# Five K pairs with seven products in nine gate/up chunks, with two weight rests per chunk on GpSimd

## The chip, the cores and the metric

The kernel runs on one core of one Trainium2 chip. The metric is the device time of one execution in microseconds, taken as the median of several runs. Before the change it is 2190.61 us (three runs, 2189.62 to 2191.96).

The engines are named as the profile names them: PE is TensorE (matrix products) and PEld its weight load, DVE the vector engine, ACT ScalarE, POOL GpSimd, SP the engine whose queue issues most transfers.

## The reference

A trunk of two layers over 256 tokens of width 2048, in float32. Each layer has a mixer (one input projection, eight heads of stick-breaking attention, eight of differential attention, one output projection) and a SwiGLU feed-forward of width 5632:

```python
for l in range(DEPTH):
    h = rms_norm(x, pre_mix_norm[l])
    m = hybrid_mixer(h, l, w_in[l], w_o[l], ...)
    x = x + rms_norm(m, post_mix_norm[l])
    h = rms_norm(x, pre_ffn_norm[l])
    f = swiglu(h, w_gate[l], w_up[l], w_down[l])
    x = x + rms_norm(f, post_ffn_norm[l])

def swiglu(h, w_gate, w_up, w_down):
    return (jax.nn.silu(h @ w_gate) * (h @ w_up)) @ w_down
```

The change concerns `h @ w_gate` and `h @ w_up`, matrices of 2048 x 5632 each.

## The kernel before

**Precision.** A float32 operand is split into a rounded part `hi` and a rest `lo` = operand - `hi`, and a product is three matmuls: hi x hi, hi x lo and lo x hi (function `product`, lines 1116 to 1118). For each weight tile of 128 x 1024, ScalarE writes `hi` (line 351) and the vector engine the rest `lo` (line 354). The rest reads two tiles in SBUF, `raw` and `hi`.

**Tiling.** The 5632 columns of gate and up are walked in eleven chunks of 512 (loop variable `c`, 0 to 10; the text calls them first to eleventh). In a chunk, K = 2048 is walked in eight pairs `kp` of two 128-row tiles. Tokens are two tiles of 128. So a pair of one chunk is a 2 x 2 block product for gate and up at once: eight products (function `eight`) or, with sums of blocks, seven (function `seven`, which calls `seven_products`). Which pairs take the second form says `gate_sevens(c)`: pairs 2, 4, 5, 6 (`SEVEN`) as a rule, 2 to 6 (`MORE_SEVEN`) in the chunks of `MORE_AT`, fewer in the first two.

**What a pair in seven products needs.** In place of two raw tiles it has `G` (gate) and `T` (up). SP's queue loads both. GpSimd issues a further transfer that adds the first half of the gate tile to the first half of `T` on the way (line 298). `feed` then takes the gate tile through lines 351 and 354 as any weight, and `mixed_weights` does the rest for the up tile: hi and lo of `T` (lines 319, 320); T's second half minus its first, in place (334); that difference added to both halves of `G`, in place (335); hi and lo of the difference (`Th`, `Tl`, 128 x 512) and of the new `G` (128 x 1024). On the token side it needs sums of token blocks, made once per layer and pair by `pair_sums` and placed by `FORM_AT`: a pair (chunk, position) gives the K pair whose sums are made there. Pairs 4, 6, 5, 2 get theirs in the first two chunks, pair 3 in the fifth.

For two pairs (3 and 5) in each of the eighth and tenth chunk the weight sums were made ahead, during the mixer's end (`foresee`, `FORESEEN`), and come back from DRAM.

**Chunk end.** After the last pair in seven products the shared sums leave PSUM (`shared_part`: line 1157 on ScalarE, 1158 to 1161 on the vector engine), after the last pair come lines 1308 to 1311 (sum, SiLU, product), and some ticks later transposes into `act` (1317, 1318).

**Order.** The program is recorded in the order of the Python code; a scheduler then orders each engine's instructions by priority and sets the semaphores. Each engine runs its queue in that order. Weights are fed four ahead of their use (`LOOKAHEAD`), the accumulating transfer of a `T` is recorded up to four weights before that (`EARLY`). There are four `raw` tiles, six `hi` and six `lo`, three `G`, four `T`, two each of `Th` and `Tl`. GpSimd's queue in the gate/up stage holds the accumulating starts and nothing else.

**x.** The residual x lies in four quarters in `rooms` (tag `late`, four places). They are written to DRAM one by one by `put_away`, in the second position of the chunks in `AWAY_AT`, which frees the places for later tiles, among them the token sums of pair 3 (`ss`).

Of the kernel before, what the change touches and what calls it, by code (L numbers as in the profile page):

```python
# [9 lines left out]
F32 = mybir.dt.float32  # L10
# [3 lines left out]
ALU = mybir.AluOpType  # L14
# [10 lines left out]
FF = 5632  # L25
CW = 512
# [18 lines left out]
FIRST_ORDER = (0, 1, 3, 2, 7, 4, 6, 5)  # L45
NEXT_SEVEN = (4, 5, 6)
MORE_SEVEN = (2, 3, 4, 5, 6)
MORE_AT = (7, 9)
FORESEEN = {7: (3, 5), 9: (3, 5)}
AHEAD_AT = 8  # L50
AHEAD_PACE = 2
FORM_AT = {(0, 1): 4, (0, 2): 6, (0, 5): 5, (1, 3): 2, (4, 3): 3}
DOWN_SEVEN = ((4, 7, 10, 12, 15, 17, 20), (3, 5, 8, 10, 13, 15, 18))

WARM = 10
LEVEL = 232
EARLY = 4
LEAD = 6
AWAY_AT = (3, 4, 5, 6)
X_BACK = 12  # L60


# [7 lines left out]
def gate_sevens(c):  # L70

    if c in MORE_AT:
        return MORE_SEVEN
# [3 lines left out]
def weight_order():  # L77

    order = []

    def queue_pair(name, l, kp, c):
        order.append((name, l, kp, c))
        return len(order) - 1

    plan = []
    sevens, plain, own = set(), set(), set()
    for l in range(L):
        lay = {"in": {}, "o": {}, "gate": {}, "up": {}, "down": {}}
        for n, (ca, cb) in enumerate(PAIRS):
            for kp in IN_ORDER if n else range(KT // 2):  # L90
                lay["in"][ca, kp] = queue_pair("w_in", l, kp, ca)
                lay["in"][cb, kp] = queue_pair("w_in", l, kp, cb)
                if kp in IN_NOW[n]:
                    plain.add(lay["in"][cb, kp])
        order_o = [(c, kp) for kp in KP_O for c in (0, 1)]
        order_o += [(c, kp) for kp in LATE_O for c in (2, 3)] + [(c, kp) for c in (2, 3) for kp in LAST_O]
        lay["order_o"] = order_o
        for c, kp in order_o:
            lay["o"][c, kp] = queue_pair("w_o", l, kp, c)
            if c == 3 and kp in O_SEVEN:  # L100
                own.add(lay["o"][c, kp])
        for c in range(FF // CW):
            for kp in FIRST_ORDER if c == 0 else range(KT // 2):
                lay["gate"][c, kp] = queue_pair("w_gate", l, kp, c)
                lay["up"][c, kp] = queue_pair("w_up", l, kp, c)
                if kp in gate_sevens(c):
                    sevens.add(lay["up"][c, kp])
        for half in range(2):
            for kp in range(FF // P // 2):
                for c in (2 * half, 2 * half + 1):  # L110
                    lay["down"][c, kp] = queue_pair("w_down", l, kp, c)
                if kp in DOWN_SEVEN[half]:
                    sevens.add(lay["down"][2 * half + 1, kp])
        plan.append(lay)
    return order, plan, sevens, plain, own
# [48 lines left out]
def kernel(  # L164
# [15 lines left out]
    nc = tc.nc  # L180
# [18 lines left out]

    order, plan, sevens, plain, own = weight_order()  # L200
    stream = [weights_in_turn[i].rearrange("p (k n) -> p k n", k=2) for i in range(len(order))]

    ready = {}
    raws, loads = [], []
    fed = [0]

    def fetch(upto):
        while len(raws) < min(upto, len(stream)):
            i = len(raws)
            for j in range(i, min(i + EARLY + 1, mix_raw[3])):  # L210
                if j in sevens and j not in sums and not (j in foreseen and j > i + 1):
                    summed(j)
            if i in sevens:
                raws.append(sums[i])
                continue
            if i + 1 in sevens:
                g = mix_raw[0].tile([P, 2, CW], F32, tag="G", bufs=mix_raw[1], name=f"G{i}")
                with not_ahead(i):
                    loads.append(nc.sync.dma_start(g, stream[i]))
                raws.append(g)  # L220
                continue
            if i in own or i + 1 in own:
                raw = mix_pool[0].tile([P, 2, CW], F32, tag="v", bufs=2, name=f"V{i}")
            elif i in plain or i + 1 in plain:
                raw = late_room([P, 2, CW], f"GU{i}")
            else:
                raw = wpool.tile([P, 2, CW], F32, tag="raw", bufs=4, name=f"raw{i}")
            mixing = bool({i, i + 1} & (own | plain))
            with not_ahead(i) if mixing else nullcontext():
                loads.append(nc.sync.dma_start(raw, stream[i]))  # L230
            raws.append(raw)
            if not mixing:
                usual.append((i, loads[-1]))
# [107 lines left out]
    def feed(upto):  # L341
        fetch(upto)
        while fed[0] < min(upto, len(stream)):
            i = fed[0]
            raw = raws[i]
            if i in sevens or i in plain or i in own:
                ready[i] = mixed_weights(i)
                fed[0] += 1
                continue
            hi = wpool.tile([P, 2, CW], F32R, tag="hi", bufs=6, name=f"hi{i}")  # L350
            nc.scalar.activation(hi, raw, AF.Copy)  # L351
            lo = wpool.tile([P, 2, CW], F32R, tag="lo", bufs=6, name=f"lo{i}")
            with behind():
                rest = nc.vector.tensor_tensor(out=lo, in0=raw, in1=hi.bitcast(F32), op=ALU.subtract)  # L354
            ready[i] = (hi, lo)
            fed[0] += 1
            rests.append(rest)
# [4 lines left out]
    def behind():  # L362

        if held[1] == 0:
            return nullcontext()
        held[1] -= 1
        return tc.issue_after(held[0].ins)

    def after_rests():

        return tc.issue_after(rests[-1].ins)
# [5 lines left out]
    def weights(i, ahead):  # L377
        feed(i + 1 + ahead)
        return ready[i]
# [20 lines left out]
    def put_away(nm, n):  # L400

        if n == 0:
            away.append(kept.tile([P, NT, D], F32, name=f"away_{nm}"))
        t, h = divmod(n, 2)
        with in_turn():
            nc.sync.dma_start(away[-1][:, t, h * D // 2 : (h + 1) * D // 2], xs[t][h])
# [760 lines left out]
    for l in range(L):  # L1167
# [17 lines left out]
        for n, (c, kp) in enumerate(plan[l]["order_o"][:16]):  # L1185
# [5 lines left out]
            if n in (9, 11):  # L1191
                kp = O_SEVEN[(n - 9) // 2]
# [4 lines left out]
        for kp in LATE_O:  # L1197
            i, j = (plan[l]["o"][c, kp] for c in (2, 3))
# [6 lines left out]
            hi, lo = weights(i, LOOKAHEAD)  # L1205
# [13 lines left out]
        with tc.manual_schedule(engines={mybir.EngineType.Activation, mybir.EngineType.DVE}):  # L1219
            feed(idx + 6)  # L1220
            for n, (c, kp) in enumerate(last_o):
                unit({0: accs[c, 0]}, mix, idx + n, kp, (0,), False, kp == LAST_O[-1], 0)
                if kp == LAST_O[-1]:
                    evac_sum(pool, accs[c, 0], mg, ssm, gpost, c, 0, f"o{l}")
            rescale(mg, ssm, 0, f"o{l}")
            for n, (c, kp) in enumerate(last_o):
                feed(idx + 7 + n)
                fetch(min(idx + 12 + n, idx + 12))
                unit({1: accs[c, 1]}, mix, idx + n, kp, (1,), False, kp == LAST_O[-1], 0)
                transposed(0, 32 + l * KT, xT, cols=(n,))  # L1230
                if (c, kp) == (2, LAST_O[-1]):
                    evac_sum(pool, accs[2, 1], mg, ssm, gpost, 2, 1, f"o{l}", True)
# [17 lines left out]
        def pair_sums(kp):  # L1250
            f = pool.tile([P, 2, S], F32, tag="t2", name=f"f{l}_{kp}")
            for kk in range(2):
                st = xT[2 * kp + kk]
                nc.vector.tensor_tensor(out=f[:, kk, :], in0=st[:, 0, :].bitcast(F32), in1=st[:, 1, :].bitcast(F32), op=ALU.add)
            forms[kp] = token_sums(pool, gu if kp in SEVEN else None, len(SEVEN), f[:, 0, 0:P], f[:, 1, 0:P], f[:, 0, P:S], f[:, 1, P:S], f"{l}_{kp}")
# [18 lines left out]
        for c in range(FF // CW):  # L1274
# [9 lines left out]
            for n, kp in enumerate(order):  # L1284
                if n == 1 and c in AWAY_AT:
                    put_away(f"ffn{l}", AWAY_AT.index(c))
                if (c, n) in FORM_AT:
                    with after_rests():
                        pair_sums(FORM_AT[c, n])
                if kp not in mine:  # L1290
# [41 lines left out]
        for half in range(2):  # L1332
# [74 lines left out]
            for t in range(NT):  # L1407
# [4 lines left out]
                for c in cc:  # L1412
                    for kp in range(nkp - tail, nkp):
# [3 lines left out]
                        hi, lo = weights(plan[l]["down"][c, kp], LOOKAHEAD)  # L1417
# [66 lines left out]
```

## Time and profile before

| | us |
|---|---|
| median of three runs | 2190.61 (2189.62 to 2191.96) |
| span of the profiled execution | 2189.2 |
| TensorE busy | 2174.7 (99%) |
| vector engine busy | 1921.7 (88%) |
| ScalarE busy | 1378.0 (63%) |
| GpSimd busy | 144.2 (7%) |
| ten gate/up chunks (second to eleventh), first layer | 418.3 |
| ten gate/up chunks, second layer | 419.0 |

How to read the profile. A group of instructions is a line of the kernel, an engine, an operation and its tiles (`lo<-raw,hi`: the output, then the inputs), their shape, a count, the busy time in us and the mean of one in ns, and behind the bar the idle time of that engine just before them with what ended it. A row of the order of time has the start in us, the duration in us, engine, line, operation; in brackets the idle time before it. A row of a table of stretches has the stretch, its length, then busy time and count for PE, PEld, DVE, ACT and POOL, the granted clock of TensorE, the DMA share and GB/s. Matmuls are pipelined and their ends modelled, so a matmul shows 0.39 us while the next one starts after 0.23 us.

### The profile page before, as it was taken

To read this page: it belongs to the slowest core of one execution; us is meant where nothing else is said; L and a number is where in the kernel's file an instruction comes from. 1 tells how busy PE (TensorE), PEld (TensorE's weight loads), DVE (VectorE), ACT (ScalarE), POOL (GpSimd) and SP (SyncE) were. 2 spreads that over 40 slices of the span, in tenths; PEclk is the share of its full clock that TensorE was granted. 3 is DMA by queue.
4 is the path that set the end of the run, shared out by engine and by line. 5 is a ranking of instruction groups with operands and counts; after the bars stand their busy time and mean duration, and the time that the engine had idled before them with its cause. 6 is when DMAs were issued, how large, how long until landed. Compare 5 with 4: busy or idle time off the path is not lost.

```text
span 2189.2 us, 28686 instructions
## 1 busy us (share of the span) xinstructions
PE 2174.7 (99%) x9980; PEld 1787.4 (82%) x9980; DVE 1921.7 (88%) x2647; ACT 1378.0 (63%) x2063; POOL 144.2 (7%) x199
## 2 busy tenths in 40 slices
PE   9999999999999999999999999999999999999998
PEld 7888888788888888888878888887788888888886
DVE  7888659999999999989878886699999999999997
ACT  7666665756656666666665656657566566666664
POOL 1100000010010000000010000000000100000000
PEclk9999999999999999999999999999999999999999
DMA  9545577587687786767465555775866877867673
GB/s 322 194 164 173 192 243 267 184 274 234 206 282 235 229 273 210 245 210 257 146 240 173 183 173 183 256 258 195 269 214 226 274 241 232 263 213 234 207 264 101
DMA packets 146033, 489.30 MB, mean 224 GB/s; under 512 B 16592, under 2 KB 17616, under 8 KB 145376
## 3 DMA queue, kind: packets, MB, share of 16 engines
q1 hardware_dynamic: 127712, 450.72, 58.9%
q0 software_dynamic: 17600, 36.22, 8.3%
q8 instruction: 78, 1.28, 0.2%
q10 hardware_dynamic: 576, 0.54, 0.1%
q14 instruction: 67, 0.55, 0.1%
HBM read 470.63 MB, written 16.78 MB: 223 GB/s over the span
## 4 chain that ended last, share of the span: by engine, by line
PE 92%; DVE 5%; ACT 1%; issue 1%; DMA 1%; DVEq 0%; ACTq 0%
PE c L1117 9%; PE c L1118 9%; PE c L1116 9%; PE in L1116 7%; PE in L1118 7%; PE in L1117 7%; PE dn L1368 4%; PE dn L1366 4%; PE dn L1365 4%; PE p L1117 2%; PE p L1118 2%; PE p L1116 2%; PE o L601 2%; PE o L603 2%; PE o L602 2%; DVE lo L354 1%
## 5 line engine op out<-in xcount | busy, mean ns | idle before, releaser
L354 DVE TENSOR_TENSOR lo<-raw,hi 128x1024 fp32r<-128x1024 f32 x514 | 615.2, 1219 | 90.7 <-ACT hi L351 89.8
L351 ACT ACTIVATE hi<-raw 128x1024 fp32r<-128x1024 f32 x514 | 531.3, 1055 | 183.1 <-DMA raw<-in_weights_in_turn_dram 51.3
L1116 PE MATMUL c<-hi,xF 128*128 128x512 f32 x806 | 317.2, 394 | 0.1
L1117 PE MATMUL c<-lo,xF 128*128 128x512 f32 x806 | 314.4, 390 | 1.2 <-DVE lo L354 1.0
L1118 PE MATMUL c<-hi,xF 128*128 128x512 f32 x806 | 314.0, 390 | 0.0
L1117 PEld LDWEIGHTS c<-lo,xF 128*128 128x128 f32 x806 | 151.5, 188 | 33.2 <-DVE lo L354 3.3
L1118 PEld LDWEIGHTS c<-hi,xF 128*128 128x128 f32 x806 | 151.3, 188 | 32.0 <-DVE xF L525 0.4
L1116 PEld LDWEIGHTS c<-hi,xF 128*128 128x128 f32 x806 | 151.4, 188 | 30.3 <-ACT xF L520 0.5
L298 POOL DMA_DIRECT2D T<-in_weights_in_turn_dram x106 | 92.2, 869 | 1257.8 <-DMA T<-in_weights_in_turn_dram 434.6
L1365 PE MATMUL dn<-hi,jh 128*128 128x512 f32 x432 | 168.2, 389 | 0.0
L1366 PE MATMUL dn<-lo,jh 128*128 128x512 f32 x432 | 168.1, 389 | 0.0
L354 DVE TENSOR_TENSOR lo<-G,hi 128x1024 fp32r<-128x1024 f32 x114 | 138.8, 1218 | 21.1 <-ACT hi L351 21.0
L319 ACT ACTIVATE hi<-T 128x1024 fp32r<-128x1024 f32 x114 | 119.7, 1050 | 41.9 <-PE c L1118 23.9
L320 DVE TENSOR_TENSOR lo<-T,hi 128x1024 fp32r<-128x1024 f32 x114 | 138.8, 1217 | 3.2 <-ACT hi L319 2.3
L351 ACT ACTIVATE hi<-G 128x1024 fp32r<-128x1024 f32 x114 | 120.0, 1053 | 30.1 <-PE c L1118 17.4
L319 ACT ACTIVATE Th<-G 128x1024 fp32r<-128x1024 f32 x106 | 111.8, 1055 | 36.8 <-DVE G L335 35.3
L320 DVE TENSOR_TENSOR Tl<-G,Th 128x1024 fp32r<-128x1024 f32 x106 | 129.1, 1218 | 5.5 <-ACT Th L319 5.3
L1368 PE MATMUL dn<-hi,jl 128*128 128x512 f32 x432 | 133.0, 390 | 0.0
L1116 PE MATMUL in<-hi,xT 128*128 128x512 f32 x328 | 131.0, 401 | 1.1 <-ACT hi L921 1.1
L1116 PE MATMUL in<-hi,xI 128*128 128x512 f32 x328 | 131.2, 401 | 0.0
L335 DVE TENSOR_TENSOR G<-G,T 128x1024 f32<-128x1024 f32 x106 | 129.3, 1220 | 1.7
L1117 PE MATMUL in<-lo,xI 128*128 128x512 f32 x328 | 128.1, 390 | 0.3 <-DVE lo L354 0.3
(485 smaller groups left out, 4786.7 us busy)
## 6 DMA issues: line engine op xcount, KB each, us to landing
raw<-in_weights_in_turn_dram SPq DMA_DIRECT2D x514, 512.0 KB, 4.7
G<-in_weights_in_turn_dram SPq DMA_DIRECT2D x114, 512.0 KB, 5.8
T<-in_weights_in_turn_dram SPq DMA_DIRECT2D x106, 512.0 KB, 6.4
T<-in_weights_in_turn_dram POOLq DMA_DIRECT2D x106, 256.0 KB, 7.2
GU<-in_weights_in_turn_dram SPq DMA_DIRECT2D x32, 512.0 KB, 6.5
Gf<-in_weights_in_turn_dram SPq DMA_DIRECT2D x8, 512.0 KB, 6.0
Tf<-in_weights_in_turn_dram SPq DMA_DIRECT2D x8, 512.0 KB, 6.7
V<-in_weights_in_turn_dram SPq DMA_DIRECT2D x8, 512.0 KB, 5.2
```

The source lines that it names most:

```text
L298: nc.gpsimd.dma_start(sums[i][:, 0, :], stream[i - 1][:, 0, :], accum_op=ALU.add)
L319: nc.scalar.activation(h, w, AF.Copy)
L320: nc.vector.tensor_tensor(out=l, in0=w, in1=h.bitcast(F32), op=ALU.subtract)
L335: nc.vector.tensor_tensor(out=g, in0=g, in1=t2.unsqueeze(1).to_broadcast([P, 2, CW]), op=ALU.add)
L351: nc.scalar.activation(hi, raw, AF.Copy)
L354: rest = nc.vector.tensor_tensor(out=lo, in0=raw, in1=hi.bitcast(F32), op=ALU.subtract)
L1116: nc.tensor.matmul(a, sh, hi, start=first, stop=False, skip_group_check=open_sums[0])
L1117: nc.tensor.matmul(a, sh, lo, start=False, stop=False, skip_group_check=open_sums[0])
L1118: nc.tensor.matmul(a, sl, hi, start=False, stop=last, skip_group_check=open_sums[0])
L1365: nc.tensor.matmul(accs[c, t], sh, hi[:, kk, :], start=first, stop=False, skip_group_check=open_sums[0])
L1366: nc.tensor.matmul(accs[c, t], sh, lo[:, kk, :], start=False, stop=False, skip_group_check=open_sums[0])
L1368: nc.tensor.matmul(accs[c, t], sl, hi[:, kk, :], start=False, stop=last, skip_group_check=open_sums[0])
```

## The change

Pairs 2 to 6 take seven products in every chunk from the third to the eleventh, not in the eighth and tenth alone. In the second to the eleventh chunk the rests of the gate tiles of pairs 1 and 2 are written by GpSimd and not by the vector engine. The token sums of pair 3 are made in the second chunk, at its sixth position, and not in the fifth. The quarters of x are put away in the second, fourth, fifth and sixth chunk; before, it was the fourth to the seventh.

```diff
-MORE_AT = (7, 9)
+MORE_AT = (2, 3, 4, 5, 6, 7, 8, 9, 10)
 FORESEEN = {7: (3, 5), 9: (3, 5)}
...
+HELPED = (1, 2)
-FORM_AT = {(0, 1): 4, (0, 2): 6, (0, 5): 5, (1, 3): 2, (4, 3): 3}
+FORM_AT = {(0, 1): 4, (0, 2): 6, (0, 5): 5, (1, 3): 2, (1, 5): 3}
...
-AWAY_AT = (3, 4, 5, 6)
+AWAY_AT = (1, 3, 4, 5)
...
+    helped = {lay["gate"][c, kp] for lay in plan for c in range(1, FF // CW) for kp in HELPED}
...
             hi = wpool.tile([P, 2, CW], F32R, tag="hi", bufs=6, name=f"hi{i}")
             nc.scalar.activation(hi, raw, AF.Copy)
             lo = wpool.tile([P, 2, CW], F32R, tag="lo", bufs=6, name=f"lo{i}")
+            if i in helped:
+                nc.gpsimd.tensor_tensor(out=lo, in0=raw, in1=hi.bitcast(F32), op=ALU.subtract)
+                ready[i] = (hi, lo)
+                fed[0] += 1
+                continue
             with behind():
                 rest = nc.vector.tensor_tensor(out=lo, in0=raw, in1=hi.bitcast(F32), op=ALU.subtract)
```

## The prediction

> **What bounds the kernel now.** I read first the page's busy times and the chain of waits, then a table of stretches cut at gate/up chunks, then the vector engine's groups in one such chunk, and last the order of time where GpSimd and the vector engine meet.
>
> ```profile
> span 2189.2 us, 28686 instructions
> ...
> PE 2174.7 (99%) x9980; PEld 1787.4 (82%) x9980; DVE 1921.7 (88%) x2647; ACT 1378.0 (63%) x2063; POOL 144.2 (7%) x199
> ...
> DVE  7888659999999999989878886699999999999997
> ...
> PE 92%; DVE 5%; ACT 1%; issue 1%; DMA 1%; DVEq 0%; ACTq 0%
> ```
>
> TensorE sets the end: 92% of the chain is its own, 5% the vector engine's. But in slices 7 to 17 and 27 to 39, which hold the gate/up stage of either layer, the vector engine is at 9 tenths. The change lives in the gate/up stage, so its price is read there. The stretches below run from one first L1308 (the gate sum that ends a chunk) to the next.
>
> ```profile
> core 0: us, PE busy (x) PEld busy (x) DVE busy (x) ACT busy (x) POOL busy (x), PEclk, DMA share, GB/s
> 439.80:484.30 44.50, 43.86 (x196) 35.46 (x195) 42.60 (x58) 26.22 (x30) 4.37 (x5) 1.00 0.81 259
> 525.10:566.90 41.80, 41.80 (x190) 34.59 (x189) 39.02 (x44) 25.30 (x29) 3.46 (x4) 1.00 0.75 241
> 733.60:775.30 41.70, 41.70 (x189) 34.56 (x188) 38.95 (x43) 25.29 (x29) 2.75 (x4) 1.00 0.76 236
> 775.30:816.40 41.10, 41.10 (x186) 34.02 (x186) 39.00 (x43) 26.78 (x31) 3.48 (x4) 1.00 0.77 253
> 439.80:858.10 418.30, 417.52 (x1877) 344.44 (x1876) 395.31 (x442) 259.33 (x300) 32.18 (x37) 1.00 0.74 238
> 1528.50:1947.50 419.00, 417.85 (x1877) 344.39 (x1876) 395.36 (x442) 258.87 (x300) 32.11 (x37) 1.00 0.74 238
> 566.90:609.90 43.00, 42.87 (x193) 35.23 (x192) 40.85 (x50) 25.81 (x30) 3.49 (x4) 1.00 0.70 217
> ```
>
> Read: the ninth chunk (733.60) has four pairs in seven products and takes 41.70 us; the tenth (775.30) has five and takes 41.10. TensorE is busy throughout in both. So one more such pair is worth 0.60 us where TensorE is the limit. The vector engine works 38.95 of the 41.70: it has 2.75 us to spare per chunk, no more. In the second chunk (439.80) it is busy 42.60 of 44.50 and TensorE already has holes. Both layers agree: 418.30 and 419.00 us for ten chunks.
>
> **The change, part by part.** Fourteen pairs (chunks three to seven, nine and eleven, two layers) go from eight to seven products: TensorE gains 14 x 0.60 = 8.4 us if nothing else takes over. What it costs the vector engine stands in its groups of the ninth chunk:
>
> ```profile
> L354 DVE TENSOR_TENSOR lo<-raw,hi 128x1024 fp32r<-128x1024 f32 x9 | 10.8, 1217 | 0.0
> L335 DVE TENSOR_TENSOR G<-G,T 128x1024 f32<-128x1024 f32 x4 | 4.9, 1223 | 0.1
> ...
> L320 DVE TENSOR_TENSOR Tl<-G,Th 128x1024 fp32r<-128x1024 f32 x4 | 4.9, 1216 | 0.0
> L320 DVE TENSOR_TENSOR Tl<-T,Th 128x512 fp32r<-128x512 f32 x4 | 2.7, 686 | 0.2 <-ACT Th L319 0.2
> L334 DVE TENSOR_TENSOR T<-T 128x512 f32<-128x512 f32 x4 | 2.7, 685 | 0.0
> ...
> L1308 DVE TENSOR_TENSOR w<-c,w 128x512 f32<-128x512 f32 x2 | 1.4, 678 | 0.0
> ```
>
> Both forms need two rests of 1.22 (L354, or L354 and L320). A pair in seven products adds L334 0.685, L335 1.223 and L320 0.686 + 1.216, in all 3.81 us. Successive instructions overlap: the 43 durations add up to some 42.9 us where the window counts 38.95 busy, 0.09 each, so the four cost 3.45. The two gate rests that leave save 2 x (1.217 - 0.09) = 2.25. Busy time of a chunk with a new fifth pair: 38.95 + 3.45 - 2.25 = 40.15 us. That alone would fit under TensorE's 41.10, with 0.95 us to spare.
>
> The two rests then run on GpSimd, which shows no operation of that size. Its nearest are the rotations (minimum, median, maximum in ns):
>
> ```profile
> L874 POOL TENSOR_TENSOR ra<-tok,rope_sb x16: 458/466/1539, 48.6 to 1235.7; 128x128 f32<-128x128 f32 x16
> L875 POOL TENSOR_TENSOR rb<-tok,rope_sb x16: 312/322/1363, 49.0 to 1237.0; 128x64 f32<-128x64 f32 x16
> ```
>
> By the medians 64 more elements take 144 ns, 2.25 ns each, so 1024 elements take 0.466 + 896 x 0.00225 = 2.5 us, of which the reading part is 1024 x 0.00225 = 2.3. The maxima matter more: the same instruction sometimes takes a microsecond longer. In order of time:
>
> ```profile
> 1141.27 1.23 DVE L354 TENSOR_TENSOR lo<-GU,hi 128x1024 fp32r<-128x1024 f32 x1 [3.66 <-ACT hi L351]
> ...
> 1141.34 1.33 POOL L875 TENSOR_TENSOR rb<-tok,rope_sb 128x64 f32<-128x64 f32 x1
> ...
> 56.08 0.46 POOL L874 TENSOR_TENSOR ra<-tok,rope_sb 128x128 f32<-128x128 f32 x1
> ...
> 56.12 1.50 DVE L320 TENSOR_TENSOR lo<-GU,hi 128x1024 fp32r<-128x1024 f32 x1 [1.13 <-ACT hi L319]
> ```
>
> At 1141.34 GpSimd starts 0.07 after a vector rest and takes 1.33 instead of 0.32: it ends 0.17 after that rest does. At 56.12 the vector engine starts 0.04 after GpSimd and takes 1.50 instead of 1.22. So two-input operations of the two engines exclude each other, whoever was first, and the loser waits about as long as the winner reads (0.28 for 128 elements is 2.2 ns each). A GpSimd rest would hold the vector engine for up to 2.3 us, and give it back 1.13.
>
> [...]
>
> How much of 2.3 is really lost? The vector engine can use the time only when idle or on operations with an input from PSUM, like L1308: 0.95 us idle and eight such operations of about 0.6 (the eight sums and differences at a chunk's end), 5.8 of 41.1. The bounds: below, 1.2 per rest, if half of it falls into that time; above, 2.4, all of it. I take 2.0, nearest to the 2.2 ns measured and one seventh hidden. So the chunk's vector time is 40.15 + 4.0 = 44.15: the vector engine becomes the bound. It cannot be filled wholly: between 0 and 1.9 us of holes (44.50 - 42.60 in the second chunk); I take 0.5, since its queue now always has work. The chunk takes 44.65, 2.95 more than 41.70, and fourteen of them +41.3 us.
>
> The eighth and tenth chunks had five such pairs already and only give away rests: 39.00 - 2.25 + 4.0 = 40.75, with 0.5 of holes 41.25: +0.2 each, four of them +0.8.
>
> The second chunk has its rests moved too, and takes over the sums for pair 3 (FORM_AT), which stood in the fifth:
>
> ```profile
> L1254 DVE TENSOR_TENSOR f<-xF 128x256 f32<-128x256 f32 x4 | 1.6, 417 | 0.0
> ...
> L1134 DVE TENSOR_TENSOR sl<-s,sh 128x512 fp32r<-128x512 f32 x2 | 1.4, 691 | 1.8 <-ACT sh L1133 1.8
> ...
> L1123 DVE TENSOR_TENSOR s<-f 128x128 f32<-128x128 f32 x2 | 0.6, 280 | 0.0
> ```
>
> One such set is 2 x 0.417 + 4 x 0.28 + 0.69 = 2.65, less 7 overlaps of 0.09, 2.0 us. Vector time there: 42.60 - 2.25 + 4.0 + 2.0 = 46.35, +3.75 on a chunk that this engine already leads: +7.5 for two. The fifth chunk gives its 2.0 back, but TensorE was the limit in its 43.00 (42.87 busy); I credit 0.5 per layer, -1.0.
>
> Moves that I cost at nothing: ScalarE gets two more splits per new pair, some 1.6 us on 25.29 of 41.70; it would cost 14 x 1.6 = 22 us if it were the limit, and it is far from it. The accumulating transfers and x's put-away:
>
> ```profile
> T<-in_weights_in_turn_dram POOLq DMA_DIRECT2D x106, 256.0 KB, 7.2
> ...
> away_ffn<-x SPq DMA_DIRECT2D x8, 512.0 KB, 8.1
> ```
>
> Fourteen more of the first and a move of the second lie under a DMA share of 0.75 to 0.81. If the put-away in the second chunk delays the weight load behind it on SP's queue by its bytes (512 KB at 259 GB/s, 2 us), two layers lose 4 us; that is the upper bound.
>
> A new wait stands on GpSimd's queue. As the changed kernel is built, the gate rest of pair 2 comes behind the accumulating starts of pairs 4 and 5, and L335 of pair 2, which overwrites the gate tile in place, waits for that rest with the whole vector queue behind it. In the fourth chunk of before the starts of pairs 4, 5 and 6 and that L335 stood at:
>
> ```profile
> 523.59 0.88 POOL L298 DMA_DIRECT2D T<-in_weights_in_turn_dram  x1 [21.97 <-DMA T<-in_weights_in_turn_dram]
> 527.38 0.87 POOL L298 DMA_DIRECT2D T<-in_weights_in_turn_dram  x1 [2.90 <-DVE w L1308]
> 531.00 0.86 POOL L298 DMA_DIRECT2D T<-in_weights_in_turn_dram  x1 [2.76 <-DMA T<-in_weights_in_turn_dram]
> ```
>
> ```profile
> 531.92 1.22 DVE L335 TENSOR_TENSOR G<-G,T 128x1024 f32<-128x1024 f32 x1
> ```
>
> Behind the start at 527.38 the rest could run from 528.3 to 530.8, 1.1 us before 531.92: just in time. With one start more ahead of it in the chunk, at the spacing of 3.6 to 3.8 shown, it would be 2.5 late. In the forecast it costs nothing, as the chunk is 3 us longer anyway.
>
> Sum: 41.3 + 0.8 + 7.5 - 1.0 = +48.6 on the profiled 2189.2 us, 2237.8. The profiled span is 1.4 below the median of the runs, 2190.61, so I predict **2239 us**.
>
> **The rivals.** (1) TensorE stays the limit: GpSimd's rests fall where the vector engine does not need the port, 40.15 fits under 41.10, and the time is 2190.6 - 8.4 = 2182. It decides where holding the port costs the vector engine less than 0.95 / 2 = 0.5 us per rest. For it: 0.95 us of slack and 4.8 us of PSUM work per chunk, and a moved rest is free to slide. Against it: the exclusion rows, both ways. [...] The row at 56.12 is a subtraction, and it was held. (2) Half of the exclusion is hidden: 1.2 per rest gives 40.15 + 2.4 = 42.55 per chunk, +0.85 x 14 = 12, the second chunk +2.15 x 2 = 4.3, less 1.0: 2206. (3) GpSimd's queue is late as well: 1.5 of the 2.5 us above in 18 chunks, +27 on the forecast: 2266. For it: the starts are spaced, and each rest may itself wait 1.2 for a vector operation. Against it: a longer chunk lets GpSimd catch up. (4) Gains and losses cancel within 4 us, near 2191: the port costs 0.8 per rest (40.15 + 1.6 = 41.75), between rivals 1 and 2.
>
> **How the numbers follow.** Forecast 0.58, rival 2 0.12, rival 3 0.16, rival 1 0.10, rival 4 0.04. A time within 0.2% (4.4 us) cannot be told from no change. Slower: 0.58 + 0.12 + 0.16 = 0.86; the same 0.04; faster 0.10. The forecast's own range is 2218 (1.6 per rest, no holes: 43.35 a chunk) to 2268 (2.4 and 1.2 of holes: 46.15 a chunk). To hold 8 in 10 it reaches to rival 2 and past rival 3: 2202 to 2276, leaving out the faster cases and a late queue at its full price.
>
> **What would show it.** Right: in the stretches of chunks three to seven, vector operations that last 2 to 3.5 us instead of 1.22, one or two per chunk and next to a GpSimd subtraction; holes in TensorE's row with the vector engine as releaser; chunks of 44 to 46 us; GpSimd subtractions of 2.5 us and, behind a vector rest, up to 3.7. Wrong: chunks at 41.1 with TensorE busy throughout (rival 1), or vector idle time that ends with GpSimd's rest at L335 (rival 3). It would be wrong altogether if vector operations kept 1.22 beside a GpSimd subtraction.

## The result and the profile after

The changed kernel takes 2218.76 us (median of four runs, 2214.95 to 2223.19) where the kernel before takes 2190.99 beside it: slower, ratio 1.0131 (95% interval 1.0119 to 1.0143), +27.8 us. The forecast was 2239, +48.6. The page of the profiled execution, span, busy times, the vector engine's slices and the chain by engine:

```profile
span 2217.6 us, 28806 instructions
...
PE 2181.5 (98%) x9938; PEld 1778.6 (80%) x9938; DVE 1960.8 (88%) x2663; ACT 1392.7 (63%) x2091; POOL 269.4 (12%) x253
...
DVE  7888669999999999989878886689999999999897
...
PE 14%; DVE 8%; issue 2%; DMA 1%; ACT 1%; DVEq 0%; SPq 0%; ACTq 0%
```

TensorE has 42 matmuls fewer (9938 for 9980), as 14 products left, and still the span is 28.4 us longer. The chain adds up to 26% of the span only, so it names no bound here, and the vector engine's slices have hardly moved: the stretches have to tell. In a table of stretches, cut at the first L1316 (the old L1308) of each chunk: the second, fifth, eighth and tenth chunk, then ten chunks of each layer.

```profile
core 0: us, PE busy (x) PEld busy (x) DVE busy (x) ACT busy (x) POOL busy (x), PEclk, DMA share, GB/s
439.30:483.50 44.20, 43.76 (x197) 35.87 (x197) 41.39 (x61) 25.29 (x30) 9.39 (x8) 1.00 0.82 271
573.30:616.00 42.70, 41.95 (x187) 33.81 (x186) 41.82 (x44) 26.59 (x31) 9.70 (x8) 1.00 0.78 242
702.00:744.90 42.90, 41.72 (x187) 33.88 (x186) 38.29 (x40) 26.15 (x31) 8.99 (x7) 1.00 0.81 269
787.80:829.50 41.70, 41.42 (x186) 33.92 (x186) 38.37 (x40) 26.38 (x31) 9.12 (x7) 1.00 0.84 276
439.30:873.80 434.50, 423.46 (x1862) 342.35 (x1862) 414.71 (x452) 267.27 (x315) 91.21 (x64) 0.99 0.75 234
1542.70:1977.40 434.70, 421.16 (x1862) 339.77 (x1861) 416.43 (x451) 267.02 (x315) 92.11 (x64) 1.00 0.75 234
```

In the fifth chunk the vector engine is busy 41.82 of 42.70 us and TensorE has holes: the bound has changed hands, as forecast. The ten chunks take 434.50 for 418.30 us. (Such a window has 1862 matmuls, 15 fewer than before, where the change takes 21 away; so six more, 1.4 us, lie inside, and the true loss is near 14.8 us in the first layer.) Chunk by chunk, in us, first layer:

| chunk | 2 | 3 | 4 | 5 | 6 | 7 | 8 | 9 | 10 | 11 |
|---|---|---|---|---|---|---|---|---|---|---|
| before | 44.51 | 40.81 | 41.77 | 43.04 | 40.88 | 41.73 | 41.09 | 41.73 | 41.08 | 41.73 |
| after | 44.19 | 46.85 | 43.04 | 42.69 | 43.11 | 42.89 | 42.87 | 42.89 | 41.70 | 44.29 |

GpSimd's rests, by groups:

```profile
L357 POOL TENSOR_TENSOR lo<-raw,hi 128x1024 fp32r<-128x1024 f32 x22 | 69.3, 3151 | 241.4 <-ACT hi L354 214.5 <-DVE Tl L323 26.9
L357 POOL TENSOR_TENSOR lo<-G,hi 128x1024 fp32r<-128x1024 f32 x18 | 45.1, 2506 | 27.3 <-issue 23.7 <-ACT hi L354 3.5
```

And what they meet, in the order of time (pair 2's rest at the start of the fifth chunk and pair 1's at its end, then, the third chunk around 502, the eighth at 723):

```profile
575.96 2.41 POOL L357 TENSOR_TENSOR lo<-G,hi 128x1024 fp32r<-128x1024 f32 x1
575.98 0.69 DVE L1318 TENSOR_TENSOR w<-c,w 128x512 f32<-128x512 f32 x1
576.77 2.15 DVE L1319 SCALAR_TENSOR_TENSOR w<-w,rs_ffn,w 128x512 f32<-128x512 f32 x1
...
610.96 1.23 DVE L362 TENSOR_TENSOR lo<-raw,hi 128x1024 fp32r<-128x1024 f32 x1
611.11 3.35 POOL L357 TENSOR_TENSOR lo<-raw,hi 128x1024 fp32r<-128x1024 f32 x1 [8.96 <-DVE Tl L323]
612.09 0.69 DVE L1166 TENSOR_TENSOR w<-p,w 128x512 f32<-128x512 f32 x1
612.89 0.69 DVE L1167 TENSOR_TENSOR w<-p,w 128x512 f32<-128x512 f32 x1
...
486.38 3.06 DVE L1319 SCALAR_TENSOR_TENSOR w<-w,rs_ffn,w 128x512 f32<-128x512 f32 x1 [0.33 <-ACT w L1317]
...
504.76 0.19 PEld L1125 LDWEIGHTS p<-Tl,ss 128*128 128x128 f32 x1 [2.49 <-DVE Tl L323]
...
723.69 1.06 ACT L322 ACTIVATE hi<-T 128x1024 fp32r<-128x1024 f32 x1 [5.29 <-DMA T<-in_weights_in_turn_dram]
724.78 1.22 DVE L323 TENSOR_TENSOR lo<-T,hi 128x1024 fp32r<-128x1024 f32 x1 [2.98 <-ACT hi L322]
```

Read: pair 2's rest runs 575.96 to 578.37. L1318, with an input from PSUM, takes its 0.69 beside it; L1319 (two inputs in SBUF) takes 2.15, not 0.74, and ends 0.55 after GpSimd does. So the exclusion that the rows of before at 1141.34 and 56.12 show for short operations is seen here for a whole rest, with 1.41 us as the price. "The port" is from here on a short name for it: the rows show that one operation waits for the other, not what the two share. Pair 1's rest comes 0.15 after a vector rest, so it is GpSimd that waits, 3.35 for 2.41, and then reads while L1166 and L1167, with PSUM inputs, take 0.69 each, as they do in before (L1158 and L1159, 0.689 and 0.691 in the mean): it costs the vector engine nothing there. The same stood in before: L1000, with an input from PSUM, takes 0.69 at 145.19 beside a GpSimd operation with two inputs in SBUF, and 0.69 is its median.

The same stretches with L1319 alone, over ten chunks:

```profile
core 0: us, DVE busy (x), PEclk, DMA share, GB/s
439.30:873.80 434.50, 30.46 (x20) 0.99 0.75 234
1542.70:1977.40 434.70, 32.09 (x20) 1.00 0.75 234
```

At the kernel before's 0.74 its twenty would take 14.8 us. The 15.7 above that belong to ten rests of pair 2: 1.57 each. In the second layer it is 17.3, in both together 33.0 us.

### The profile page after: what moved, and what is told of

It reads as the page before. It is cut to its first block, busy times and chain, and to the rows that moved or that the text cites. A ratio compares the mean times of both kernels' runs of the same rounds, so it can differ in the third digit from the quotient of the medians.

```text
span 2217.6 us, 28806 instructions
## 1 busy us (share of the span) xinstructions
PE 2181.5 (98%) x9938; PEld 1778.6 (80%) x9938; DVE 1960.8 (88%) x2663; ACT 1392.7 (63%) x2091; POOL 269.4 (12%) x253
## 5 line engine op out<-in xcount | busy, mean ns | idle before, releaser
L362 DVE TENSOR_TENSOR lo<-raw,hi 128x1024 fp32r<-128x1024 f32 x464 | 558.6, 1223 | 97.2 <-ACT hi L354 96.2
L354 ACT ACTIVATE hi<-raw 128x1024 fp32r<-128x1024 f32 x486 | 501.3, 1055 | 167.5 <-DMA raw<-in_weights_in_turn_dram 80.8
L1124 PE MATMUL c<-hi,xF 128*128 128x512 f32 x708 | 279.1, 395 | 0.1
L1125 PE MATMUL c<-lo,xF 128*128 128x512 f32 x708 | 276.1, 390 | 1.0 <-DVE lo L362 1.0
L1126 PE MATMUL c<-hi,xF 128*128 128x512 f32 x708 | 275.9, 391 | 0.0
L322 ACT ACTIVATE Th<-T 128x512 fp32r<-128x512 f32 x120 | 75.5, 629 | 168.7 <-DVE T L337 168.7
L323 DVE TENSOR_TENSOR lo<-T,hi 128x1024 fp32r<-128x1024 f32 x128 | 156.3, 1221 | 11.0 <-ACT hi L322 10.8
L1125 PEld LDWEIGHTS c<-lo,xF 128*128 128x128 f32 x708 | 133.0, 188 | 28.9 <-DVE lo L362 2.8
L1126 PEld LDWEIGHTS c<-hi,xF 128*128 128x128 f32 x708 | 132.9, 188 | 28.3 <-DVE xF L533 0.5
L1124 PEld LDWEIGHTS c<-hi,xF 128*128 128x128 f32 x708 | 133.0, 188 | 26.5 <-ACT xF L528 0.5
L323 DVE TENSOR_TENSOR Tl<-G,Th 128x1024 fp32r<-128x1024 f32 x120 | 146.8, 1223 | 4.6 <-ACT Th L322 4.4
L338 DVE TENSOR_TENSOR G<-G,T 128x1024 f32<-128x1024 f32 x120 | 146.9, 1224 | 2.9 <-issue 0.4
L354 ACT ACTIVATE hi<-G 128x1024 fp32r<-128x1024 f32 x128 | 134.8, 1053 | 10.6 <-DMA G<-in_weights_in_turn_dram 7.7
L1124 PE MATMUL in<-hi,xT 128*128 128x512 f32 x328 | 131.3, 402 | 0.4 <-ACT hi L929 0.4
L1124 PE MATMUL in<-hi,xI 128*128 128x512 f32 x328 | 131.1, 401 | 0.0
```

Of the source, the lines that this page charges most:

```text
L322: nc.scalar.activation(h, w, AF.Copy)
L323: nc.vector.tensor_tensor(out=l, in0=w, in1=h.bitcast(F32), op=ALU.subtract)
L338: nc.vector.tensor_tensor(out=g, in0=g, in1=t2.unsqueeze(1).to_broadcast([P, 2, CW]), op=ALU.add)
L1124: nc.tensor.matmul(a, sh, hi, start=first, stop=False, skip_group_check=open_sums[0])
L1125: nc.tensor.matmul(a, sh, lo, start=False, stop=False, skip_group_check=open_sums[0])
L1126: nc.tensor.matmul(a, sl, hi, start=False, stop=last, skip_group_check=open_sums[0])
```

## The experiments

Times are medians, each with its ratio to the kernel before on the same chip (2189.6 to 2190.1 us there). A diff stands against the changed kernel unless it says otherwise.

**No GpSimd rests** (e1) and **the port taken out** (e3).

```diff
# e1
-HELPED = (1, 2)
+HELPED = ()
# e3
-nc.gpsimd.tensor_tensor(out=lo, in0=raw, in1=hi.bitcast(F32), op=ALU.subtract)
+nc.gpsimd.memset(lo.bitcast(F32), 0.0)
+nc.gpsimd.tensor_tensor(out=lo[:, :, 0:8], in0=raw[:, :, 0:8], in1=hi.bitcast(F32)[:, :, 0:8], op=ALU.subtract)
```

> The changed kernel with all rests back on the vector engine. Theory A, the vector engine is the bound and the two GpSimd rests give it back only 2.25 - 1.75 = 0.5 us per chunk: its time per chunk with five pairs is 38.95 + 3.45 = 42.4, with 1.0 of holes 43.4, 0.5 more than the 42.9 of the changed kernel, over 14 chunks and a little in the third, 2226 to 2232 us. Theory B, the GpSimd rests themselves (port and queue) cause the loss: without them 2190 to 2210 us.

> The changed kernel, but GpSimd fills the two rests with zeros and subtracts only 16 of 1024 elements: 98% of these two rests is left out. The queue and the waits on both operands stay, GpSimd hardly reads SBUF. Theory A, the port: vector time falls by 1.4 to 1.8 us per chunk to 40.2 to 40.5, below TensorE's 41.1; chunks of 41.2 to 41.8, 2196 to 2204 us. Theory B, late accumulated tiles in GpSimd's queue or the five pairs in a row: no more than 0.5 us per chunk comes back, 2210 us or more.

Measured: without GpSimd rests 2213.56 us, ratio 1.0110 (1.0095 to 1.0125), which neither theory had. With rests that hardly read, 2185.94, ratio 0.9985 (0.9976 to 0.9995), better than either theory. Stretches of that kernel, ten chunks and the fifth:

```profile
438.80:856.50 417.70, 415.96 (x1863) 341.11 (x1862) 399.88 (x452) 271.70 (x316) 67.22 (x82) 1.00 0.78 244
565.30:606.50 41.20, 41.20 (x187) 33.97 (x186) 40.43 (x45) 27.19 (x31) 7.70 (x9) 1.00 0.82 248
```

The fifth chunk's vector time is 40.43, and TensorE has no holes in it. So reading through the port costs 2218.8 - 2185.9 = 32.8 us, 0.82 for each of 40 rests, and turns a gain of 3.7 us into a loss of 27.8. (Counted from the kernel before as it was measured beside each, it is 27.8 + 3.7 = 31.5; the kernel before differed by 1.4 us there.) The seven products alone, without help, cost 23 us: the help gains 27.6 and the port takes 32.8. The rest cut down is also shorter on GpSimd, 1.0 + 0.5 to 0.9 us for 2.4, so a part of the 32.8 could be GpSimd's own time; but the 33.0 us by which L1319 alone is longer in the changed kernel speak for the port.

**Which rest pays** (e8: pair 2's rest cut down in that way; e9: pair 1's).

```diff
+light = {lay["gate"][c, 2] for lay in plan for c in range(1, FF // CW)}   # e8; 1 in place of 2 for e9
...
+if i in light:
+    nc.gpsimd.memset(lo.bitcast(F32), 0.0)
+    nc.gpsimd.tensor_tensor(out=lo[:, :, 0:8], in0=raw[:, :, 0:8], in1=hi.bitcast(F32)[:, :, 0:8], op=ALU.subtract)
+else:
     nc.gpsimd.tensor_tensor(out=lo, in0=raw, in1=hi.bitcast(F32), op=ALU.subtract)
```

> The changed kernel, but GpSimd's rest of pair 2 is a fill with zeros and a subtraction of 16 of its 1024 elements; pair 1's is whole. The vector engine's order is that of the changed kernel, so the result splits the 32.8 us that the port cost in all into the two pairs. Theory A (pair 2's rest, which holds the product after the chunk's end, is what costs): 2186 to 2194 us. Rival B (both pairs cost about alike): 2199 to 2206 us. Rival C (pair 1's is what costs): 2212 us or more.

> The mirror of the run with pair 2's rest cut down: pair 1's rest is a fill with zeros and a subtraction of 16 of 1024 elements, pair 2's is whole. Theory A: 2211 to 2219 us. Rival B: 2199 to 2206 us. Rival C: 2186 to 2194 us.

Measured: 2190.04 us (ratio 1.0000, 0.9991 to 1.0009) and 2216.30 (1.0120, 1.0105 to 1.0134). Theory A holds in both: pair 2's rests cost 28.7 us, 1.44 each, pair 1's 2.5, 0.12 each, which is not clear of the spread of the runs (2214.95 to 2223.19 us for the changed kernel, 2210.95 to 2220.83 for e9). Start of a chunk with pair 2's rest cut down, in the order of time (its L1324 is L1319), and ten chunks of L1324 alone:

```profile
569.74 0.74 DVE L1324 SCALAR_TENSOR_TENSOR w<-w,rs_ffn,w 128x512 f32<-128x512 f32 x1
...
569.90 1.28 POOL L359 MEMSET lo<- 128x1024 f32 x1
```

```profile
439.60:858.90 419.30, 14.94 (x20) 1.00 0.77 242
```

14.94 for 30.46: the 1.57 per rest are gone, and the ten chunks are 15.2 us shorter. The eighth chunk, whose loss had looked like a late `T`, went from 42.87 to 41.05 us with it (in the second layer from 42.69 to 42.10).

**One rest alone** (e5: pair 1; e12: pair 1, cut down; e10: pair 2).

```diff
-HELPED = (1, 2)
+HELPED = (1,)      # e5; e12 with the cut-down rest; (2,) in e10
```

> The changed kernel with pair 2's gate rest back on the vector engine; pair 1's stays on GpSimd (20 GpSimd rests instead of 40). Theory A (pair 1's rest runs at the chunk's end beside the operations with an input from PSUM and costs about nothing, while pair 2's holds the subtraction or product that follows the chunk's end for 1.4 us or more and gives back only 1.13): 2200 to 2208 us, vector time about 41 us in a chunk with five pairs, and the operations of line 1319 at 0.74 us. Rival B (the price per rest is the same for both pairs, about 0.8 us each): 2213 to 2219 us, between the changed kernel and the one without GpSimd rests.

> The kernel with pair 1's gate rest alone on GpSimd (2228.9 us), with that rest cut down to a fill with zeros and a subtraction of 16 of 1024 elements. It asks why one moved rest made the kernel slower than none (2213.6) and than two (2218.8). Theory A (the port: here pair 1's GpSimd rest falls beside a vector rest of two SBUF inputs, two of which take 4.56 us in place of 2.36 in the order of time): the vector rests go back to 1.22 and the time to 2190 to 2207 us. Rival B (the queues: pair 1's rest waits on GpSimd for its hi half, the accumulating starts behind it are late, and the loads of T and G with them, port or not): 2215 to 2229 us.

> The changed kernel with GpSimd rests for pair 2 alone; pair 1's are back on the vector engine. It is the fourth corner beside none (2213.6), pair 1 alone (2228.9) and both (2218.8). Theory A (each corner has an order of its own on the vector engine, and the time is set by what the port meets in that order and by when the G tiles come free, so that the pairs' prices do not add): outside of 2200 to 2208. Rival B (the prices add: with pair 1 +15.3, both +5.2, so pair 2 alone -10.1): 2203.5, 2200 to 2208 us.

| GpSimd writes | us | ratio (95%) | pair 1's rest cut down |
|---|---|---|---|
| no rest | 2213.56 | 1.0110 (1.0095 to 1.0125) | |
| pair 1 | 2228.87 | 1.0180 (1.0163 to 1.0197) | 2220.18, 1.0137 (1.0121 to 1.0154) |
| pair 2 | 2201.82 | 1.0055 (1.0040 to 1.0071) | |
| both | 2218.76 | 1.0131 (1.0119 to 1.0143) | 2216.30, 1.0120 (1.0105 to 1.0134) |

Both of my expectations for e5 were far off, theory A by 20 us: moving pair 1's rest alone, which was cheap at the port beside pair 2's, makes the kernel slower, by 15.3 us, and moving the dear one alone makes it 11.7 faster. The prices of the two moves add to within 2 us (2217.1 by addition, 2218.8 measured): e10 falls into the band of its rival B, and theory A of it, that they would not add, falls. e12 falls into the band of its rival B, but the port makes the larger part of pair 1's price when alone: 8.7 of the 15.3 us go with the rest cut down, 6.6 stay. The 8.7 stand in the order of time of e5. There pair 1's rest falls beside two vector rests, which take 4.56 us in place of 2.36 (vector engine, then GpSimd):

```profile
1722.88 4.56 DVE L362 TENSOR_TENSOR lo<-raw,hi 128x1024 fp32r<-128x1024 f32 x2
...
1723.89 2.46 POOL L357 TENSOR_TENSOR lo<-raw,hi 128x1024 fp32r<-128x1024 f32 x1 [11.28 <-ACT hi L354]
```

The second layer has four such rows, 4 x 2.2 = 8.8 us, the first none; and only the second layer's ten chunks are shorter in e12 (435.7 us for 443.7). So pair 1's rest is not cheap in itself: its price follows from what it meets.

No run isolates the cause of the 6.6 that stay. But the mean granted clock of TensorE is 0.999 in e1's profile and 0.995 in e12's (0.994 or 0.995 in all four runs of e12, 0.997 to 0.999 in those of e1). That is 0.4% of 2218 us, 9 us as an estimate, and enough to cover the 6.6; the last section shows a lower clock behind two holes of four.

Two more things show in the traces. First, where pair 2's gate rest is the vector engine's, loads of `G` come late: ScalarE waits for them 56.1 us in e1, 40.1 in e5 and 40.3 in e12, but 9.2 in the changed kernel, 10.6 in e10 and 8.1 in e3. (As e1 has the most, this is not what makes pair 1 alone slower than none.) Waits of e12, then of the changed kernel (total us, times, longest):

```profile
ACT hi L354 <- DMA G<-in_weights_in_turn_dram: 40.3, 22, 4.0
```

```profile
ACT hi L354 <- DMA G<-in_weights_in_turn_dram: 9.2, 11, 1.5
```

The order of time of e12 in the sixth chunk has the chain (there are three `G` tiles, and the load could start once `Tl` had been taken from one of them; L1125 of e12 is L1124 of the changed kernel):

```profile
633.69 1.22 DVE L323 TENSOR_TENSOR Tl<-G,Th 128x1024 fp32r<-128x1024 f32 x1
...
634.94 0.33 SPq L222 DMA_DIRECT2D G<-in_weights_in_turn_dram  x1
...
640.58 1.06 ACT L354 ACTIVATE hi<-G 128x1024 fp32r<-128x1024 f32 x1 [1.56 <-DMA G<-in_weights_in_turn_dram]
...
643.58 0.50 PEld L1125 LDWEIGHTS p<-Th,sh 128*128 128x128 f32 x2 [3.46 <-ACT Th L322]
```

The load is issued 0.03 us after that subtraction ends, is taken up 5.64 later, and TensorE has stood for 3.46 us when the pair's `Th` is there. Second, in pair 1's absence pair 2's GpSimd rest comes earlier. Order of time of e10, and its ten chunks of L1319 alone:

```profile
571.00 0.68 DVE L1316 TENSOR_TENSOR w<-c,w 128x512 f32<-128x512 f32 x1
571.61 0.68 DVE L1318 TENSOR_TENSOR w<-c,w 128x512 f32<-128x512 f32 x1
572.20 0.68 DVE L1316 TENSOR_TENSOR w<-c,w 128x512 f32<-128x512 f32 x1
572.80 1.73 DVE L1319 SCALAR_TENSOR_TENSOR w<-w,rs_ffn,w 128x512 f32<-128x512 f32 x1
...
571.23 2.75 POOL L357 TENSOR_TENSOR lo<-G,hi 128x1024 fp32r<-128x1024 f32 x1
```

```profile
439.40:864.13 424.73, 23.30 (x20) 1.00 0.76 239
```

It starts 0.23 us after the chunk's first L1316, not 2.61 as in the changed kernel (575.96 and 573.35), and operations with PSUM inputs lie beside its first part. Over the ten chunks L1319 loses 0.85 per rest (23.30 - 14.8, by ten) instead of 1.57. The mean hides two cases, in both layers: in the third to eighth chunk the rest starts within 0.5 us of that L1316 and L1319 loses 0.4 to 1.3, in the ninth to eleventh it starts 1.5 to 2.7 behind and L1319 loses 1.5 to 1.7 (in the second it loses nothing). Over both layers L1319 takes 62.6 us in the changed kernel and 47.4 in e10, 15.1 of the 17 us between the two. In the changed kernel pair 1's rest and two accumulating starts run on GpSimd just ahead of pair 2's (568.09, 572.48 and 575.03), in e10 one start (570.67); that this order alone sets the later start is not shown.

**The rests alone** (e2) and **the placement alone** (e6), both against the kernel before.

```diff
# e2, with the branch in feed
+HELPED = (1, 2)
# e6
-FORM_AT = {(0, 1): 4, (0, 2): 6, (0, 5): 5, (1, 3): 2, (4, 3): 3}
+FORM_AT = {(0, 1): 4, (0, 2): 6, (0, 5): 5, (1, 3): 2, (1, 5): 3}
-AWAY_AT = (3, 4, 5, 6)
+AWAY_AT = (1, 3, 4, 5)
```

> The kernel before with pairs 1 and 2 of the gate on GpSimd in the second to eleventh chunk, nothing else of the change. Theory A: a chunk's vector time is 38.95 - 2.25 + 1.75 = 38.45, under TensorE's 41.70, so nothing is lost; the second chunk gains up to 0.5 us: 2189 to 2192 us, with the chunk-end product (mean 0.74 us alone) at 2.0 us or more once per chunk. Theory B: rests that come late behind GpSimd's starts hold TensorE by 0.5 us or more in 20 chunks: 2200 us or more.

> The kernel before with the two moves of the change alone: pair 3's token sums in the second chunk, and x's first quarter put away in the second chunk. Theory A (the sums cost the second chunk about 2 us per layer and the fifth gives back 1 to 2, the put-away is covered): 2190 to 2195 us. Rival B (the put-away delays the weight loads behind it on SP's queue and the sums are late for the third chunk): 2198 us or more, with TensorE holes in the second and third chunks.

Measured: 2193.51 us (ratio 1.0016, 1.0007 to 1.0026) and 2189.71 (0.9998, 0.9989 to 1.0008). Stretches of e2, the second, fourth, eighth and tenth chunk, then of e6, the second and third:

```profile
439.70:482.00 42.30, 42.17 (x190) 34.61 (x189) 40.44 (x55) 26.23 (x30) 12.06 (x9) 1.00 0.82 274
523.80:565.50 41.70, 41.70 (x189) 34.56 (x188) 38.35 (x41) 25.23 (x29) 8.37 (x6) 1.00 0.75 238
691.20:733.70 42.50, 41.43 (x187) 33.86 (x186) 38.38 (x41) 26.05 (x31) 8.75 (x5) 1.00 0.72 233
775.40:818.50 43.10, 41.66 (x186) 33.88 (x186) 38.38 (x40) 26.05 (x31) 8.83 (x5) 1.00 0.71 234
```

```profile
440.70:484.00 43.30, 42.41 (x189) 34.45 (x189) 41.23 (x61) 25.46 (x30) 3.48 (x4) 1.00 0.70 230
484.00:526.20 42.20, 42.20 (x191) 34.77 (x190) 41.92 (x46) 26.36 (x30) 4.36 (x5) 1.00 0.82 281
```

With four pairs in seven products the rests cost nothing in the fourth chunk (41.70, TensorE full) and take 2.2 us off the second, of which the third gives 1.0 back; they lose 1.4 and 2.0 in the eighth and tenth (41.09 and 41.08 before), the two with five pairs (0.9 and 0.2 in the second layer). So e2 lies between its theories. e6 lies just under its theory A. The placement is free: 85.5 us for the second and third chunk against 85.3 before.

**Two versions to gain by it.** e4 has both rests of pair 1 (gate and up) on GpSimd and none of pair 2's. e7 has that in the second to seventh and the ninth chunk, five pairs in the fourth to tenth alone, pair 3's sums in the third.

```diff
# e4
-HELPED = (1, 2)
+HELPED = (1,)
-helped = {lay["gate"][c, kp] for lay in plan for c in range(1, FF // CW) for kp in HELPED}
+helped = {lay[m][c, kp] for lay in plan for m in ("gate", "up") for c in range(1, FF // CW) for kp in HELPED}
# e7, besides
-MORE_AT = (2, 3, 4, 5, 6, 7, 8, 9, 10)
+MORE_AT = (3, 4, 5, 6, 7, 8, 9)
+HELPED_AT = (1, 2, 3, 4, 5, 6, 8)                # in place of the range
...(1, 5): 3 becomes (2, 5): 3; AWAY_AT = (2, 3, 4, 5)
```

> The changed kernel with GpSimd on both rests of pair 1 (gate and up) in place of the gate rests of pairs 1 and 2. Pair 1's gate rest runs beside the chunk-end operations with an input from PSUM in the changed kernel and holds nothing up. Theory A: the up rest follows it and holds up the vector engine for less than the 1.4 us of pair 2's, by 0 to 1.0, so 0.4 to 1.4 us per chunk come back: 2200 to 2212 us. Theory B, where a rest stands does not matter: 2215 to 2223 us.

> Built from what the runs showed: five pairs in seven products in the fourth to tenth chunk, pair 3's sums in the third chunk, the put-away in the third to sixth, and GpSimd's rests those of pair 1 alone (gate and up) in the second to seventh and the ninth chunk. Theory A (GpSimd's rests of pair 1 are nearly free, and the losses of the changed kernel sat in the second, third, eighth and eleventh chunk, which this kernel leaves as they were before): 2184 to 2190 us, a little faster than before. Rival B (two rests of pair 1 still cost 0.5 to 1 us of vector time in each such chunk, so TensorE's 0.6 us per pair is not reached): 2193 to 2200 us.

Measured: 2200.31 us (1.0047, 1.0032 to 1.0062) and 2191.26 (1.0008, 0.9999 to 1.0018). e4 lies at the lower edge of its theory A, e7 between its two and no better than before.

**What is left over** (e11, e7 cut to the part that had gained).

```diff
# against e7
-MORE_AT = (3, 4, 5, 6, 7, 8, 9)
+MORE_AT = (7, 9)
-HELPED_AT = (1, 2, 3, 4, 5, 6, 8)
+HELPED_AT = (1,)
```

> The kernel before with what the runs showed to gain: in the second chunk alone the rests of pair 1 (gate and up) on GpSimd, pair 3's sums in the third chunk and not in the fifth, x put away in the third to sixth chunk; five pairs in seven products only in the eighth and tenth chunk, as before. Theory A (the second chunk gains 2 us per layer as in the kernel with hidden rests, the third and fifth together about 0): 2185 to 2188 us. Rival B (the gain is given back in the chunk behind): 2189 to 2192 us.

Measured: 2187.07 us, ratio 0.9987 (0.9978 to 0.9995): a little faster than the kernel before, in the band of theory A. Its second and third chunk:

```profile
440.60:483.30 42.70, 42.57 (x192) 34.94 (x191) 41.83 (x56) 26.11 (x30) 7.59 (x7) 1.00 0.82 276
483.30:526.20 42.90, 42.90 (x194) 35.51 (x193) 40.97 (x51) 26.26 (x31) 3.12 (x4) 1.00 0.68 220
```

44.50 became 42.70 where the vector engine had led. But the third chunk, which makes pair 3's sums here, went from 40.81 to 42.90, so the two together take 85.6 us for 85.3; the fourth and fifth are 1.3 us shorter each, the sixth 0.9 longer, and the ten chunks take 417.0 for 418.3. e11 moves rests, sums and put-away at once, so it does not show which of them gains. That moved rests help in the second chunk is seen in e2, whose second and third chunk take 84.1 us with nothing else moved.

## Why the forecast was right in direction and too high in size

- **TensorE's gain, 8.4 us.** With the port's cost gone (e3), 3.7 us of it come out.
- **Vector time 40.15 without the port.** Right: 40.43 in e3.
- **A GpSimd rest of 2.5 us.** Right: 2.41 alone, 3.35 behind a vector rest. 3.7 had been given as the most; two rests, those at the end of the first chunk in either layer, took 3.97 and 3.90.
- **The two engines exclude each other for the whole read.** Right, shown by e3 and e8: L1319 at 2.15 goes back to 0.75.
- **2.0 us per rest, "nearest to the 2.2 ns measured and one seventh hidden".** This is the term that was mis-sized: 0.82 (32.8 / 40). The share hidden was worked out as if rests fell anywhere in a chunk. They do not: `hi` of pair 1 is ready at the end of a chunk and `hi` of pair 2 at the start of the next, which is where the operations with PSUM inputs stand. Pair 1's is hidden nearly whole (0.12, no more than the runs' spread), pair 2's by about a third (1.44 left). The fifth chunk's vector time is 41.82, 1.39 over e3's, where 4.0 was forecast.
- **Holes of 0.5 per chunk.** Too small: 42.70 - 41.82 = 0.9 and, in the eighth chunk, 4.6 of vector idle time, part of it as `T` came late.
- **Second chunk +3.75, eighth and tenth +0.2, fifth -0.5.** The second is 0.3 shorter in the first layer and 1.4 in the second. Pair 3's sums cost nothing over the second and third chunk (e6). The moved rests, with the port, do not shorten it: without them (e1) it takes 42.82 and 44.11 us, with them 44.19 and 43.81. In their place stands the third chunk, +6.0 and +6.6, with 43.50 us of vector work in the first layer, an L1319 of 3.06 and later a hole of 2.49 in TensorE; with the port taken out (e3) it takes 42.64 and 43.00, so 4.2 and 4.4 of its loss are the port's. The eighth lost 1.8, the tenth 0.6.

With the measured 0.82 in its formula the forecast would have been 40.15 + 1.64 + 0.5 = 42.29 a chunk and 2201 us in all (+8.3 for fourteen chunks, +2.8 for the second, -1.0). The 18 us up to 2218.8 are what the formula had no term for: per chunk against it, the third +9.6 in two layers, the ten chunks four to seven and nine +6.7, the eighth and tenth +4.5, the eleventh +4.0, the second -3.8, less 2.8 for the matmuls that only moved into the window. So the forecast's range held through two errors of opposite sign, which is luck in part. Of the rivals, rival 4 had the right price (0.8) and the wrong time, since it let a chunk of 41.75 us of vector work last 41.75; rival 3 did not come: the waits have no row in which the vector engine waits for GpSimd's `lo`; rival 1's condition, under 0.5 per rest, is missed by pair 2's rest alone.

Not settled: 34 us separate e12 from e3, which differ in where pair 2's gate rest is written, with neither kernel reading much through the port. In TensorE it shows as longer waits for `Th` (30.0 us for 2.1) and as the lower clock. Behind that can stand the vector work that the moved rest takes off, 20 x 1.13 = 22.6 us, or the late loads of `G`; a fourth `G` tile wasn't tried, so the two are not told apart.

## What to carry to other kernels

When GpSimd takes over an elementwise operation with SBUF inputs, do not price the port by an average: look at which vector operations will stand beside it. Here a rest beside operations with an input from PSUM was nearly free (0.12 us, e9); beside one that reads two SBUF tiles it cost 1.4 us (e8), and beside two vector rests 2.2 (e5). A nearly full engine also left holes in the engine it feeds before it was the limit by its busy time: in e12 a ring of three tiles refilled late, and TensorE stood for 3.46 us, with the vector engine at 41.05 of 45.20 us. Moved work paid where the loaded engine led, as in the second chunk of e2 (42.30 us for 44.51), and changed nothing where TensorE led, as in its fourth (41.70 for 41.77).

## What was not expected of the hardware

After the hole of 2.49 us in the third chunk the granted clock was halved. Stretches of the changed kernel before, in and after it:

```profile
501.00:505.00 4.00, 1.93 (x9) 1.31 (x8) 4.00 (x5) 2.90 (x4) 0.00 (x0) 1.00 0.70 184
505.00:508.40 3.40, 3.40 (x9) 2.71 (x9) 3.40 (x5) 1.41 (x2) 0.87 (x1) 0.51 0.61 185
508.40:512.00 3.60, 3.60 (x17) 2.88 (x17) 3.60 (x4) 3.56 (x5) 0.00 (x0) 0.98 0.92 219
```

Nine matmuls in 3.40 us, where 0.227 each would have let fifteen through: the hole cost another 1.4 us. (2.49 is the hole of the weight loads; TensorE's matmuls, with their modelled ends, leave one of 2.07.) The same place of the second layer has a hole of 2.50, and no lower clock behind it:

```profile
1608.10:1611.50 3.40, 3.40 (x15) 2.83 (x16) 3.40 (x5) 1.25 (x2) 0.87 (x1) 1.00 0.58 192
```

In e12 it is the same: no lower clock behind a hole of 3.41 that ends at 555.75, but one behind a hole of 3.46 that ends at 643.58: 13 matmuls and a clock of 0.67 in its 8 us, for 23 and 1.00 in the other's:

```profile
552.00:560.00 8.00, 5.01 (x23) 3.82 (x22) 7.55 (x9) 6.43 (x7) 0.85 (x1) 1.00 0.59 166
640.00:648.00 8.00, 4.96 (x13) 3.59 (x12) 6.99 (x8) 5.45 (x7) 0.87 (x1) 0.67 0.64 169
```

So holes of nearly one length have a lower clock behind them (2.49 and 3.46 us) or none (2.50 and 3.41); what decides it is not shown. The changed kernel's slow stretch is the 3.40 us at 0.51 above; from 508.40 on the clock is 0.98.

The second surprise was that the price of a GpSimd rest goes with its start: in e10 0.4 to 1.3 us of L1319 where it starts within 0.5 us of the chunk's first L1316, 1.5 to 1.7 where it starts 1.5 to 2.7 behind.
